# The delta-rule heads' outputs turned by VectorE in 32x32 blocks instead of by TensorE, and attention outputs multiplied by their reciprocals one visit later

## The chip, the core and the metric

The kernel runs on one core of a Trainium2 chip. The metric is the device time of one execution in microseconds (us). The three runs of the kernel before took 1198.80, 1198.78 and 1195.98 us; their median is 1198.78 us.

## The reference, cut to what matters

One decoder layer over 1024 tokens of width 1024, all in float32:

```python
h = rmsnorm(x, norm1_w);  proj = h @ w_in                 # q, k, v, z, gates | q, k, v of attention
o_a = gated_delta_rule(q, k, v, g, beta)                  # 4 heads x 128
o_a = rmsnorm(o_a, gdn_norm_w) * silu(z)
o_b = dilated_attention(q_b, k_b, v_b)                    # 8 heads x 64, numerator / denominator
x = x + concat([o_a, o_b]) @ w_out
h = rmsnorm(x, norm2_w);  u = causal_dwconv(h @ w_up)
x = x + (silu(gate) * up) @ w_down;  out = rmsnorm(x, final_norm_w)
```

The delta rule is a recurrence over chunks of tokens for each of the four heads. Its result `o_a` has tokens on the rows; the output projection wants it with the 128 features of a head on the partitions, so each head's 128 x 1024 result has to be turned once.

## The kernel before, in words

All large matrix products run on TensorE as three products of split operands (high and low parts), each 128x512 out: one "triple" is `xhi,whi`, `xlo,whi`, `xhi,wlo`. The order of TensorE's instructions is the order in which the Python program writes them: every `mm` and `tp` gets an order token. That program is a set of generators (streams) which the class `Weave` interleaves by its own estimate of time: `dense` (level 9, the input projection, the filler), `chain(h)` (level 1, the recurrence of head h), `attention` (level 5), and later `out_proj`, `mlp_up`, `mlp_down`. VectorE, ScalarE, GpSimd and the SyncE queue (SP, which issues nearly all DMAs) have no tokens: there a list scheduler places each instruction where it reckons the engine free and the operands ready, and the order in which the program writes them only ranks what is ready at once. Engines `uv` and `ua` give their instructions a rank 400 places ahead. Every engine then runs its queue in order.

Names used below, with the lines of before:

- `chain(h)` (847): for each of 8 chunks a loop through two engines: `mm(kT, st)`, then VectorE makes `r`, `mm(um, r)`, VectorE makes `wke` and ScalarE copies `w`, `mm(ktok, wke)`, VectorE makes the new state `ct`, and so on. Beside it `vtok` collects the output. All four heads run at once, 0 and 1 ahead of 2 and 3. At the end `ms` (911) is raised to -0.5 on GpSimd, and GpSimd multiplies `vtok` by it (912, 913).
- `finish(h)` (916): turns `vtok` of a head in two halves. Four 128x128 transposes on TensorE go into one bank of PSUM (`tag "atr"`), ScalarE copies the bank to `ot` with the scale `gw2`, and a DMA writes `ot` to the DRAM tensor `mixer`. `ot` has two buffers under the tag `t2`, shared with `oT` and `rT`.
- `dense()` (535): after the values and the q and v columns come eight attention columns `a` and four columns `z`. A column is 16 triples in two halves of eight; each half ends in a bank with tag `hf` (two buffers) which VectorE empties (`aqkv`, 1.10 us). Column `z` of head h waits for `finish(h)` (588), loads `og` back from `mixer` (613) and multiplies it by the gate (614).
- `attention()` (949) waits for all four `finish`. Its work is cut in visits (`advance`, 1095): in a visit the newest pair of blocks is turned (`turn`, 1006: transposes of `sm`, copies to `pt` and `pb`), the pair before it is multiplied with the values, and the next pair's scores go to `softmax` (990: VectorE's fused maximum, ScalarE's exponentials). At every second visit a group is complete; `give` (1080) multiplies its bank `po` with `rT`, the reciprocals of the denominators, which VectorE turned (`dt`, 1035, a 128x32 block transpose) and a DMA through `ddram` spread over the partitions.

Of the kernel before, what the change touches and what calls it, by code (L numbers as in the profile page):

```python
# [7 lines left out]
F32 = mybir.dt.float32  # L8
F32R = mybir.dt.float32r
AF = mybir.ActivationFunctionType  # L10
# [137 lines left out]
def hybrid_layer(tc, I, out):  # L148
# [113 lines left out]
    atpark = dp.tile([H, P, S], F32, name="atpark")  # L262
    ddram = dp.tile([7, 8, P], F32, name="ddram")
    ndram = dp.tile([S], F32, name="ndram")
    xpark = dp.tile([KT, P, S], F32, name="xpark")
    upark = dp.tile([FT, P, S], F32, name="upark")

# [3 lines left out]
    def next_bank(tag, *tiles, slack=0.0):  # L271

        while max(wv.need(*tiles), wv.slot_free(tag, 2)) + slack > 1e-3:
            yield max(wv.need(*tiles), wv.slot_free(tag, 2)) + slack
        return bank(tag)
# [239 lines left out]
    def silu2(xr, name):  # L515
        y = A(name, "ev")
        ac.activation(y, xr, AF.Tanh, scale=0.5)
        ve.scalar_tensor_tensor(y, y, 1.0, xr, op0=OP.add, op1=OP.mult)
        return y
# [15 lines left out]
    def dense():  # L535

        yield from wv.until("first")
        yield from wv.until("norms")
        wv.add(2, first_keys())

        srcs, tiles = [], 0
        for col in DENSE:
            if col[0] == "V":
                srcs += [I["wv"][j] for j in range(4)]
            else:
                srcs.append(I["wi"][tiles])
                tiles += 1
        place = [0]
        raw = [raw_weight(srcs[0])]
        nxt = [weight(None, st=raw.pop())]  # L550
        raw.append(raw_weight(srcs[1]))

        def take():
            w = nxt.pop()
            i = place[0] = place[0] + 1
            if i < len(srcs):
                nxt.append(weight(None, st=raw.pop(), spare=i >= 17))
            if i + 1 < len(srcs):
                raw.append(raw_weight(srcs[i + 1]))
            return w  # L560

        def values_by_token(g):

            banks = [bank(t) for t in ("asc", "asc", "ch", "ch")]
            for j in range(4):
                w = [t.rearrange("p (k m) -> p k m", k=2) for t in take()]
                for kk in range(2):
                    k = 2 * j + kk
                    for i, pt in enumerate(banks):
                        c = 4 * g + i  # L570
                        yield wv.need(pt, *w)
                        mm3(pt, [t[:, c * P:(c + 1) * P] for t in xs[k]], [t[:, kk, :] for t in w], k == 0, k == KT - 1)
            for i in range(0, 4, 2):
                vx = A("vx", "ev", shape=(P, 2, 512))
                for e in range(2):
                    c = 4 * g + i + e
                    ac.activation(vx[:, e, :], banks[i + e], AF.Copy, scale=rst[:, c:c + 1])
                c = 4 * g + i
                sy.dma_start(vpark[c * P:(c + 2) * P].rearrange("(e p) d -> p e d", e=2), vx)
            wv.done.add(("V", g))  # L580

        for i, col in enumerate(DENSE):
            kind, h = col[:2]
            if kind == "V":
                yield from values_by_token(h)
                continue
            if kind == "z":
                yield from wv.until(("o", h))
            w = [t.rearrange("p (k m) -> p k m", k=KT) for t in take()]
            pair = []  # L590
            for hh in range(2):
                pt = bank("hf")
                yield wv.need(pt, *w)
                for k in range(KT):
                    mm3(pt, [t[:, k, :] for t in w], [t[:, half(hh)] for t in xs[k]], k == 0, k == KT - 1)
                    yield 0.0

                pair.append(pt)
                if hh == 0:
                    xr = A("aqkv" if kind == "a" else "xr", "go" if kind == "k" else "ev")  # L600
                scaled(pair, "xr", kind == "a", t=xr, hs=(hh,))
            if kind == "k":
                T["k", h] = conv_silu(xr, 4 + h, "kT", "kT*")
                wv.add(3, kprep(h))
            elif kind == "q":
                q = conv_silu(xr, h, "qT", "qa")
                wv.add(4, qprep(h, q))
            elif kind == "v":
                v = conv_silu(xr, 8 + h, "vT", "qa")
                wv.add(4, vprep(h, v))  # L610
            elif kind == "z":
                og = gated[h] = A("og", "kT*")
                sy.dma_start(og, mixer[h])
                ve.tensor_tensor(og, og, silu2(xr, "zz"), op=OP.mult)
            else:
                sy.dma_start(apark[h, col[2]], xr)
                wv.done.add(col)
        wv.done.add("dense")
# [295 lines left out]
        wv.add(1, finish(h, vtok))  # L914

    def finish(h, osb):
        for hh in range(2):
            pt = yield from next_bank("atr", osb)
            for c in range(4):
                i = 4 * hh + c  # L920
                tp(pt[:, c * P:(c + 1) * P], osb[:, i * P:(i + 1) * P])
            ot = tile_(sp, [P, 512], F32, "ot", "t2", 2)
            ac.activation(ot, pt, AF.Copy, scale=gw2)
            sy.dma_start(mixer[h][:, half(hh)], ot)
        wv.done.add(("o", h))


# [21 lines left out]
    def attention():  # L949
# [56 lines left out]
        def turn(pair):  # L1006
            pts = A("pt", "dv*", shape=(P, 2, 2, 256))
            for b, (it, tag) in enumerate(zip(pair, ("asc", "atr"))):
                sm, near, far, u, den = it["sm"], it["near"], it["far"], it["u"], it["den"]
                nn, nf = near // P, -(-far // P)  # L1010
                pt = it["pt"] = pts[:, b]
                pps = [bank(tag) for _ in range(2)]
                pvs = [pp.rearrange("p (e i t) -> p e i t", e=2, t=64) for pp in pps]
                for e in range(2):
                    for i in range(nn + nf):
                        o = far + i * P if i < nn else (i - nn) * P
                        for pv, rr in zip(pvs, HALVES):
                            tp(pv[:, e, i, :], sm[rr, e, o:o + P], ident[rr, rr], 0.055)
                copies = uv.tensor_copy, lambda dst, src: ua.activation(dst, src, AF.Copy)
                for pv, rr, copy in zip(pvs, HALVES, copies):  # L1020
                    copy(pt.rearrange("p e (i t) -> p e i t", t=P)[:, :, :nn, rr], pv[:, :, :nn, :])
                    for i in range(nf):
                        rows = min(it["far"] - i * P, P)
                        copy(it["pb"][i][:rows, :, u, rr], pv[:rows, :, nn + i, :])
                g = it["g"]
                if g["n"] < 7:
                    uv.reciprocal(dns[g["n"] % 2][:, 2 * u:2 * u + 2], den)
                    continue
                rd = it["rd"] = tile_(sp, [P, P], F32, "rd", ("r0", "r1", "w0", "w1")[u], 1)
                uv.reciprocal(den, den)  # L1030
                po_.tensor_copy(rd.rearrange("p (e d) -> p e d", e=2), den[:, :, None].to_broadcast([P, 2, 64]))
            g = pair[0]["g"]
            if g["n"] < 7 and pair[1]["u"] == 3:
                dt = tile_(sp, [P, 32], F32, "dt", "dt", 2)
                ve.transpose(dt, dns[g["n"] % 2])
                to = ddram[g["n"]]
                for b in range(4):
                    sq.dma_start(to[:, 32 * b:32 * b + 32], dt[32 * b:32 * b + 8, :])
                rT = g["rT"] = tile_(sp, [P, 512], F32, "rT", "t2", 2)
                for e, er in enumerate(HALVES):  # L1040
                    src = to.rearrange("(u e) t -> e u t", e=2)[e]
                    sq.dma_start(rT[er].rearrange("p (u t) -> p u t", u=4),
                                 bass.AP(tensor=src.tensor, offset=src.offset, ap=[[0, 64]] + list(src.ap)))
# [47 lines left out]


        pipe = [None, None]

        def advance(pair):
            older, newer = pipe
# [8 lines left out]
                yield from spread(older)  # L1105
            if newer is not None:
                turn(newer)
            if older is not None:
                yield from values(older)
                if older[1]["u"] == 3:  # L1110
                    yield from merge_classes(g)
                    give(g)
            if pair is not None:
                yield from scores(pair, 0.3 if older is None else SSLACK)
            pipe[:] = newer, pair
# [599 lines left out]
```

## Time and profile before

| what | value |
|---|---|
| median of three runs | 1198.78 us |
| the profiled execution's own time | 1197.6 us |
| its span, first to last instruction | 1195.7 us |
| granted TensorE clock, mean | 0.997 |
| TensorE busy | 1183.4 us, 99% of the span |
| VectorE busy | 914.6 us, 76% |
| ScalarE busy | 571.6 us, 48% |
| DMA moved | 157.20 MB, 131 GB/s |

A timeline row gives start, duration, engine, line, operation, the tiles written and read, and a count; what stands in brackets is idle time before the row and who ended it. Matmuls overlap in the pipeline: a 128x512 product is shown with some 0.39 us, but the next starts 0.23 us after it. What an instruction costs TensorE is therefore read from one start to the next. Lines 142, 144, 194 and 198 are those of the helpers that issue instructions, so rows are told apart by their tiles.

### The profile page before, as it was taken

The page shows a single profiled execution, that of the slowest core. Times are in us where ns is not written, and L with a number is a line of the kernel's source. Part 1 is how long each engine was busy: PE and PEld are TensorE (multiplying, and loading weights), DVE is VectorE, ACT ScalarE, POOL GpSimd, SP SyncE. Part 2 cuts the span into 40 slices and gives each one's busy share as a digit, 9 for nine tenths or more (in the row PEclk, how much of TensorE's full clock was granted, in tenths as well). Part 3 has the DMA queues.
Part 4 walks back from the last instruction along what each step waited for, and adds up shares of the span by engine and source line. Part 5 has one row for each costly group of instructions (what it writes and reads, how often), then busy time and mean ns, then how long its engine had stood idle before and what let it go on. Part 6 is the DMA issues. An engine that isn't in the chain of part 4 may idle for free.

```text
span 1195.7 us, 18250 instructions
## 1 busy us (share of the span) xinstructions
PE 1183.4 (99%) x7014; PEld 977.9 (82%) x7014; DVE 914.6 (76%) x1457; ACT 571.6 (48%) x1119; POOL 81.9 (7%) x74
## 2 busy tenths in 40 slices
PE   9999999999999999999999999999999999999997
PEld 6888888888777778888888888888888888888886
DVE  6683975666365665777898898989889889999875
ACT  7275345355444533655554444445444453434441
POOL 0212010214211110000000000000000000000000
PEclk9999999999999999999999999999999999999998
DMA  7435234435644214443322312132231398546514
GB/s 238 107 96 146 79 118 129 145 120 176 223 133 133 90 49 129 166 159 106 106 79 79 104 55 106 53 106 76 83 104 56 123 359 293 194 153 224 169 53 141
DMA packets 90263, 157.20 MB, mean 131 GB/s; under 512 B 21920, under 2 KB 40640, under 8 KB 90176
## 3 DMA queue, kind: packets, MB, share of 16 engines
q1 hardware_dynamic: 89312, 155.25, 39.8%
q8 instruction: 55, 0.90, 0.3%
q10 hardware_dynamic: 864, 0.79, 0.2%
q14 instruction: 32, 0.26, 0.1%
HBM read 120.04 MB, written 35.96 MB: 130 GB/s over the span
## 4 chain that ended last, share of the span: by engine, by line
PE 95%; ACT 2%; DVE 2%; issue 1%; DMA 0%; POOLq 0%; POOL 0%; DVEq 0%; SPq 0%; ACTq 0%
PE ps L194 45%; PE pa L194 20%; PE dw L194 17%; PE pc L194 10%; PE ps L198 2%; DVE kT L142 1%; ACT sm L144 1%; DMA xt<-in_xT 0%; ACT whi L142 0%; DVE x1h L142 0%; DVE zz L142 0%; ACT dec L142 0%; PE pd L194 0%; DVE xr L142 0%; DVE sm L144 0%
## 5 line engine op out<-in xcount | busy, mean ns | idle before, releaser
L194 PE MATMUL dw<-pr 128*128 128x512 f32 (+1 forms) x984 | 211.9, 377 | 0.0
L194 PEld LDWEIGHTS dw<-pr 128*128 128x128 f32 x984 | 176.5, 188 | 34.4 <-DVE x1h L142 0.4
L194 PE MATMUL ps<-xhi,whi 128*128 128x512 f32 x384 | 157.1, 409 | 1.2 <-ACT xhi L144 1.2
L194 PE MATMUL ps<-xhi,wlo 128*128 128x512 f32 x384 | 150.1, 391 | 0.0
L194 PE MATMUL ps<-xlo,whi 128*128 128x512 f32 x384 | 148.4, 390 | 0.0
L194 PE MATMUL pa<-T,pair 128*128 128x512 f32 x528 | 127.1, 390 | 0.1
L194 PEld LDWEIGHTS pa<-T,pair 128*128 128x128 f32 x528 | 99.0, 188 | 20.9 <-ACT u L142 0.5
L194 PEld LDWEIGHTS ps<-xhi,whi 128*128 128x128 f32 x384 | 72.2, 188 | 20.1 <-issue 5.6
L194 PEld LDWEIGHTS ps<-xhi,wlo 128*128 128x128 f32 x384 | 72.1, 188 | 15.5
L194 PEld LDWEIGHTS ps<-xlo,whi 128*128 128x128 f32 x384 | 72.3, 188 | 12.7 <-DVE xlo L144 0.2
L142 ACT ACTIVATE u<-pa 128x512 f32<-128x512 f32 x44 | 26.3, 599 | 107.8 <-PE pa L194 107.8
L142 DVE SCALAR_TENSOR_TENSOR y<-xu,fcw,y 128x1023 f32<-128x1023 f32 (+1 forms) x44 | 56.4, 1281 | 23.3 <-ACT y L142 23.2
L142 ACT ACTIVATE whi<-wst 128x1024 fp32r<-128x1024 f32 x36 | 38.2, 1062 | 65.2 <-PE ps L194 43.4
L194 PE MATMUL pa<-T,S 128*128 128x512 f32 x264 | 63.5, 389 | 0.0
L194 PE MATMUL pc<-T,S 128*128 128x512 f32 x264 | 63.4, 389 | 0.0
L194 PE MATMUL pa<-B,A 128*128 128x512 f32 x264 | 63.4, 389 | 0.0
L194 PE MATMUL pc<-B,pair 128*128 128x512 f32 x264 | 63.4, 389 | 0.0
L142 ACT ACTIVATE pr<-r 128x1024 fp32r<-128x1024 f32 (+1 forms) x44 | 36.6, 840 | 51.5 <-PE dw L194 29.8
L142 DVE TENSOR_TENSOR wst<-wst 128x512 f32<-128x512 f32 x88 | 60.5, 687 | 0.8
L194 PE MATMUL ps<-B,pair 128*128 128x512 f32 x252 | 60.5, 389 | 0.0
L194 PEld LDWEIGHTS pa<-T,S 128*128 128x128 f32 x264 | 49.5, 188 | 10.5 <-ACT p L142 0.2
L194 PEld LDWEIGHTS pc<-T,S 128*128 128x128 f32 x264 | 49.6, 188 | 10.3
(253 smaller groups left out, 2325.0 us busy)
## 6 DMA issues: line engine op xcount, KB each, us to landing
wst<-in_wu SPq DMA_DIRECT2D x44, 512.0 KB
wd<-in_wd SPq DMA_DIRECT2D x44, 512.0 KB
upark<-y SPq DMA_DIRECT2D x22, 512.0 KB
wst<-in_wi SPq DMA_DIRECT2D x21, 512.0 KB
r<-upark SPq DMA_DIRECT2D x11, 512.0 KB
r<-upark SPq DMA_DIRECT2D x22, 256.0 KB
wa<-in_wd SPq DMA_DIRECT2D x22, 256.0 KB
wst<-in_wv SPq DMA_DIRECT2D x8, 512.0 KB
```

Source lines behind the costliest of these rows:

```text
L142: return getattr(eng, op)(*a, **kw)
L144: return getattr(eng, op)(*a, **kw)
L194: tc.stamp_issue_order_token(nc.tensor.matmul(dst, lhs, rhs, start=start, stop=stop, **kw).ins, TOKEN)
L198: tc.stamp_issue_order_token(nc.tensor.transpose(dst, src, ident if idt is None else idt).ins, TOKEN)
```

## The change

Four edits.

1. `finish` no longer uses TensorE, the bank and ScalarE. VectorE transposes each 128x128 piece of `vtok` in 32x32 blocks (`ve.transpose`) straight to `ot`; four DMAs for each half put the blocks in their places in a new DRAM tensor `odram`, each in 512 runs of 128 B; four DMAs for each head read `og` back in runs of 512 B. The scale `gw2` moves to the gate's multiplication, which becomes a `scalar_tensor_tensor`.
2. `finish` yields until the chains of heads 2 and 3 are written.
3. In `turn`, the rows that make and spread the reciprocals (`dt`, `ddram`, `rT`) become a function `rows_out` of their own.
4. `give` of a group is put on a list and written one visit later, between `turn` and `rows_out`; the last two groups keep their place.

```diff
+    odram = dp.tile([H, 32, 4 * S], F32, name="odram")
...
                 og = gated[h] = A("og", "kT*")
-                sy.dma_start(og, mixer[h])
-                ve.tensor_tensor(og, og, silu2(xr, "zz"), op=OP.mult)
+                of = odram[h].rearrange("j (c a t) -> a j c t", c=NCH, a=4)
+                for a in range(4):
+                    sq.dma_start(v8(og)[32 * a:32 * a + 32], of[a])
+                ve.scalar_tensor_tensor(og, og, gw2, silu2(xr, "zz"), op0=OP.mult, op1=OP.mult)
...
     def finish(h, osb):
+        for i in (2, 3):
+            yield from wv.until(("c", i, NCH - 1))
+        yield wv.need(osb)
         for hh in range(2):
-            pt = yield from next_bank("atr", osb)
+            yield 0.3
+            ot = tile_(sp, [P, 512], F32, "ot", "t2", 2)
             for c in range(4):
-                i = 4 * hh + c
-                tp(pt[:, c * P:(c + 1) * P], osb[:, i * P:(i + 1) * P])
-            ot = tile_(sp, [P, 512], F32, "ot", "t2", 2)
-            ac.activation(ot, pt, AF.Copy, scale=gw2)
-            sy.dma_start(mixer[h][:, half(hh)], ot)
+                ve.transpose(ot[:, c * P:c * P + P], osb[:, (4 * hh + c) * P:(4 * hh + c + 1) * P])
+            to = odram[h].rearrange("j (f b i) -> b j f i", f=32, b=4)[:, :, 16 * hh:16 * hh + 16]
+            for b in range(4):
+                sq.dma_start(to[b], ot[32 * b:32 * b + 32].rearrange("p (f i) -> p f i", i=32))
...
+        def rows_out(pair):
             g = pair[0]["g"]
...
+            while ungiven:
+                give(ungiven.pop())
+            if newer is not None:
+                rows_out(newer)
...
-                    give(g)
+                    if g["n"] < 6:
+                        ungiven.append(g)
+                    else:
+                        give(g)
```

On TensorE the 32 transposes `ps<-ident,vtok` are gone and nothing else is added or removed. The attention's visits stand five triples later among the dense work (its first scores after 275 triples instead of 270), and from the triple numbered 321 on the two orders are the same.

VectorE, where the last chunks of heads 2 and 3 are done (`ps_2456`, and `ps_2457` after the change, is the bank of head 2; `ps_2466` and `ps_2467` that of head 3). Before:

```order
L142 TENSOR_SCALAR ms_2447<-ms_2447 128x8
L144 SCALAR_TENSOR_TENSOR vtok_2413<-ps_2962,gq_2327,vtok_2413 128x128
L142 TENSOR_TENSOR aqkv_2980<-ps_2650,rstdB_245 128x4x32x4
L144 TENSOR_SCALAR wke_2974<-ps_2456,ke_1096 128x128
L144 SCALAR_TENSOR_TENSOR r_2978<-ps_2466,ngam_248,vtok_2413 128x128
```

and after, at the same place (`vtok_1483` is the output of head 0):

```order
L142 TENSOR_SCALAR ms_2448<-ms_2448 128x8
L142 STREAM_TRANSPOSE ot_3151<-vtok_1483 128x128
L144 SCALAR_TENSOR_TENSOR vtok_2414<-ps_2963,gq_2328,vtok_2414 128x128
L142 STREAM_TRANSPOSE ot_3151<-vtok_1483 128x128 x2
L142 TENSOR_TENSOR aqkv_2981<-ps_2651,rstdB_246 128x4x32x4
L142 STREAM_TRANSPOSE ot_3151<-vtok_1483 128x128
L144 TENSOR_SCALAR wke_2975<-ps_2457,ke_1097 128x128
L144 SCALAR_TENSOR_TENSOR r_2979<-ps_2467,ngam_249,vtok_2414 128x128
```

The first four transposes stand ahead of head 2's `wke` and head 3's `r`, though the program writes them after both chains.

VectorE, at the last `ct` and `r` of head 3 (chunk 7). Before:

```order
L144 SCALAR_TENSOR_TENSOR ct_2432<-ct_2432,ge_630,ps_2466 128x128
L144 SCALAR_TENSOR_TENSOR vtok_2413<-ps_3126,gq_2327,vtok_2413 128x128
L144 SCALAR_TENSOR_TENSOR r_3142<-ps_2466,ngam_248,vtok_2413 128x128
L142 TENSOR_TENSOR aqkv_3177<-ps_3106,rstdB_245 128x4x32x4
L144 SCALAR_TENSOR_TENSOR vtok_2413<-ps_3167,gq_2327,vtok_2413 128x128
```

and after (`vtok_2030` is the output of head 2, `vtok_1713` that of head 1):

```order
L142 STREAM_TRANSPOSE ot_3169<-vtok_2030 128x128
L144 SCALAR_TENSOR_TENSOR ct_2433<-ct_2433,ge_631,ps_2467 128x128
L142 STREAM_TRANSPOSE ot_3169<-vtok_2030 128x128 x3
L142 STREAM_TRANSPOSE ot_3181<-vtok_1483 128x128 x4
L144 SCALAR_TENSOR_TENSOR vtok_2414<-ps_3104,gq_2328,vtok_2414 128x128
L142 TENSOR_TENSOR aqkv_3117<-ps_3063,rstdB_246 128x4x32x4
L144 SCALAR_TENSOR_TENSOR r_3115<-ps_2467,ngam_249,vtok_2414 128x128
L142 STREAM_TRANSPOSE ot_3190<-vtok_1713 128x128 x4
L144 SCALAR_TENSOR_TENSOR vtok_2414<-ps_3138,gq_2328,vtok_2414 128x128
```

Seven transposes and an `aqkv` now stand between head 3's last `ct` and its last `r`, and one transpose of head 2's output ahead of that `ct`. On GpSimd a weight's low part (`wlo`) now stands between the power of head 2's `ms` and the multiplication of its `vtok`.

VectorE in the attention, at the first `oT`. Before:

```order
L144 COPY pt_3522<-ps_3542 128x4x64
L144 COPY pb_3400<-ps_3542 128x2x64
L142 TENSOR_TENSOR oT_3577<-ps_3416,rT_3462 128x4x4x32
L144 ISA sm_3596,mx_3597<-ps_3580,mk_2953 128x416
L144 ISA mx_3597 128x1
```

and after:

```order
L144 COPY pt_3546<-ps_3566 128x4x64
L144 COPY pb_3424<-ps_3566 128x2x64
L142 TENSOR_TENSOR oT_3715<-ps_3443,rT_3489 128x4x4x32
L144 ISA sm_3617,mx_3618<-ps_3601,mk_2954 128x416
L144 ISA mx_3618 128x1
```

The multiplication keeps its place in VectorE's queue, between the copies of one visit and the maxima of the same visit; only its tile is numbered later, because it is written later.

More of the change, by code (lines that the diff above doesn't have):

```diff
@@ L1093, in attention @@
         pipe = [None, None]
+        ungiven = []
         def advance(pair):
```

## The prediction

> **What bounds the kernel now.** I read the page first, then the table of windows around the changed stage, then the timelines of TensorE, VectorE and GpSimd in it. From the page, the busy times and the chain that ended last:
>
> ```profile
> PE 1183.4 (99%) x7014; PEld 977.9 (82%) x7014; DVE 914.6 (76%) x1457; ACT 571.6 (48%) x1119; POOL 81.9 (7%) x74
> PE 95%; ACT 2%; DVE 2%; issue 1%; DMA 0%; POOLq 0%; POOL 0%; DVEq 0%; SPq 0%; ACTq 0%
> ```
>
> TensorE is busy 1183.4 of 1195.7 us and holds 95% of the chain, so the time is TensorE's work plus its few waits. The windows of the stage in which the chains end and the attention begins (columns: stretch, length, then busy time and count of each engine, clock, DMA share, GB/s):
>
> ```profile
> 270.00:290.00 20.00, 19.41 (x146) 17.93 (x145) 13.66 (x45) 13.12 (x52) 7.38 (x5) 1.00 0.54 163
> 290.00:310.00 20.00, 20.00 (x109) 17.13 (x108) 6.65 (x15) 7.97 (x20) 10.01 (x7) 1.00 0.73 224
> 310.00:330.00 20.00, 20.00 (x168) 15.27 (x166) 7.61 (x30) 8.99 (x26) 4.75 (x2) 1.00 0.67 231
> ```
>
> TensorE hardly waits here. VectorE (third pair) is busy 13.66, 6.65 and 7.61 of 20 us: it has room for more, but its instructions are steps of the chains for which TensorE waits, so the place of new work counts more than its amount.
>
> **What leaves TensorE.** The 32 transposes stand in six places of TensorE's timeline, each quoted with the row that follows:
>
> ```profile
> 284.48 1.03 PE L198 MATMUL ps<-ident,vtok 128*128 128x128 f32 x8
> 285.35 0.39 PE L194 MATMUL ps<-wke,ktok 128*128 128x128 f32 x2
> ...
> 287.61 0.39 PE L194 MATMUL ps<-w,qat 128*128 128x128 f32 x2
> 288.12 0.63 PE L198 MATMUL ps<-ident,vtok 128*128 128x128 f32 x4
> 288.58 0.39 PE L194 MATMUL ps<-ct,kT 128*128 128x128 f32 x2
> ...
> 289.73 0.60 PE L198 MATMUL ps<-ident,vtok 128*128 128x128 f32 x4
> 290.08 0.48 PE L194 MATMUL ps<-xhi,whi 128*128 128x512 f32 x1
> 290.40 0.40 PE L194 MATMUL ps<-xlo,whi 128*128 128x512 f32 x1
> 290.63 0.40 PE L194 MATMUL ps<-xhi,wlo 128*128 128x512 f32 x1
> ...
> 298.87 0.60 PE L198 MATMUL ps<-ident,vtok 128*128 128x128 f32 x4
> 299.31 0.39 PE L194 MATMUL ps<-ct,kT 128*128 128x128 f32 x2
> ...
> 300.23 0.60 PE L198 MATMUL ps<-ident,vtok 128*128 128x128 f32 x4
> 300.58 0.48 PE L194 MATMUL ps<-xhi,whi 128*128 128x512 f32 x1
> ...
> 310.92 1.03 PE L198 MATMUL ps<-ident,vtok 128*128 128x128 f32 x8
> 311.71 0.48 PE L194 MATMUL ps<-xhi,whi 128*128 128x512 f32 x1
> ```
>
> From start to start: 0.87, 0.46, 0.35, 0.44, 0.35, 0.79, together 3.26. Where a 128x512 product follows, its own pace is spoiled too: 290.08 to 290.40 is 0.32, against 0.23 for the next, so 0.09 goes with each of the three places where the transposes alone broke a run of triples: 0.27. And ahead of 288.12 stands a wait: the pair before it started at 287.61 and such a pair takes 0.22 (285.35 ends a run in which pairs follow at that pace), so 0.29 goes. The sum is 3.82 us, all of it on the path. It would be no gain only where TensorE waits in its place, which is the next term. ScalarE's eight copies of `ot` go too; ScalarE is busy 7.97 of 20 us there, so I count nothing for them.
>
> **What VectorE gets.** 32 transposes of 128x128. The trace has none of that size; the nearest is the one of 128x32, and steps of the chain show what a 128x128 operation takes. VectorE's and GpSimd's timelines, around the first and the second place of the order:
>
> ```profile
> L142 DVE STREAM_TRANSPOSE dt<-dn x7: 211/211/213, 328.5 to 417.4; 128x32 f32<-128x32 f32 x7
> 283.54 1.10 DVE L142 TENSOR_TENSOR aqkv<-ps,rstdB 128x512 f32<-128x512 f32 x1
> 284.48 0.33 DVE L144 TENSOR_SCALAR wke<-ps,ke 128x128 f32<-128x128 f32 x1
> 284.72 0.34 DVE L144 SCALAR_TENSOR_TENSOR r<-ps,ngam,vtok 128x128 f32<-128x128 f32 x1
> ...
> 298.63 0.35 DVE L144 SCALAR_TENSOR_TENSOR ct<-ct,ge,ps 128x128 f32<-128x128 f32 x1 [1.26 <-PE ps L194]
> 299.74 0.34 DVE L144 SCALAR_TENSOR_TENSOR r<-ps,ngam,vtok 128x128 f32<-128x128 f32 x1
> 281.26 1.90 POOL L142 TENSOR_TENSOR vtok<-vtok,ms 128x1024 f32<-128x1024 f32 x1
> 293.13 1.64 POOL L142 TENSOR_TENSOR ms<-ms,mhalf 128x8 f32<-128x8 f32 x1 [1.24 <-DVE ms L142]
> 296.70 2.38 POOL L142 TENSOR_TENSOR wlo<-wst,whi 128x1024 fp32r<-128x1024 f32 x1
> ```
>
> A transpose lies between 0.21 (a quarter of the columns) and 0.84 (four times that). I take 0.26 from start to start: 128x128 operations follow each other after 0.24 (284.48 to 284.72), and the 128x32 transpose with its 0.211 is already near them. The Trainium skill, "VectorE: DVE Perf Modes", section "The three transpose paths", gives 311 ns on VectorE and 390 ns on TensorE for a 128x128 bf16 transpose; by 0.31 the waits below would grow by 16 x 0.05 = 0.8 us.
>
> First place: head 0's `vtok` is ready at 281.26 + 1.90 = 283.16, as VectorE gets there. Four transposes push `wke` from 284.48 to 285.52, and it ends at 285.52 + 0.33 = 285.85. TensorE now has two triples before the product that needs it. With a triple of 3 x 0.23 and 0.09 for the change of kind they take 1.45 from 283.70, where such a product starts in before's timeline, so TensorE arrives at 285.15 and **waits 0.7 us** (from 0, if transposes take 0.21 and the ends overlap, to 1.9, if GpSimd's rough span ends as late as the transposes at 284.48 allow).
>
> ```profile
> 283.56 0.39 PE L194 MATMUL ps<-ct,kT 128*128 128x128 f32 x2
> 283.70 0.47 PE L194 MATMUL ps<-xhi,whi 128*128 128x512 f32 x1
> ```
>
> Next come four transposes ahead of head 3's `ct`; with two triples on TensorE before the product that reads it, I find `ct` done as TensorE arrives: 0.
>
> Second place: head 2's multiplication on GpSimd now comes after a `wlo`: 293.13 + 1.64 + 2.38 + 1.90 = 299.05. The one transpose ahead of `ct` waits for it, and `ct` starts at about 299.5 instead of 298.63; TensorE, which has more triples in front, reads it at 300.1 and does not notice. But between `ct` and `r` stand seven transposes, a `vtok` and an `aqkv`: 0.26 + 7 x 0.26 + 0.26 + 0.94 (283.54 to 284.48) = 3.28, and `r` ends 0.35 later, 3.63 after `ct` starts. TensorE has its pair (0.14) and three triples (3 x 0.68 + 0.09 = 2.13) from 300.1, so it wants `r` at 302.4 and gets it at 303.15: it **waits 0.8 us** (0 to 2.5, by transposes of 0.21 and of about half the upper price).
>
> After that no chain is left. TensorE has 22 triples (15 us) before the first scores, and the remaining 16 transposes, 4.2 us, lie beside them. What they can hold up there is `aqkv`, which frees the bank that TensorE needs eight triples (5.4 us) later. That cover is gone only if the transposes themselves wait, which is a rival below.
>
> **DMA queue.** SP issues 32 + 16 DMAs instead of 8 + 4. The nearest shapes, in runs of 128 B:
>
> ```profile
> 173.94 1.91 SPq L142 DMA_DIRECT2D x<-xdram  x4
> 175.96 3.88 SPq L142 DMA_DIRECT2D um<-xtdram  x8
> 300.70 0.38 SPq L142 DMA_DIRECT2D wst<-in_wi  x1
> 322.12 1.04 ACT L142 ACTIVATE whi<-wst 128x1024 fp32r<-128x1024 f32 x1
> ```
>
> At 0.48 each that is 36 x 0.48 = 17 us more of SP's time between 285 and 330. Behind them are weights: the one loaded at 300.70 is first read at 322.12, so a delay of some us there is covered by 20 us. `og` is read only after 410 us. I count 0.
>
> **Later multiplication.** The order shows `oT` unmoved in VectorE's queue, so this part does not do what it says; 0. What moves in the attention is ScalarE's `whi`: it stood between two exponentials of a visit in which TensorE then waited, and stands now between two of another visit.
>
> ```profile
> PE ps L198 <- ACT sm L144: 0.8, 4, 0.2
> ```
>
> These waits are 0.8 us in all. I take 0, with bounds of 0.8 on both sides.
>
> **Sum.** -3.82 + 0.7 + 0.8 = -2.3 us. Against the profiled execution (1197.6 with a span of 1195.7, 1.9 us lying around it) that makes 1195.3. The median of the runs is 1198.78, 1.2 above the profiled one; from it, **1196.5 us**, 0.19% faster. That is less than 0.3% (3.6 us), about what a measurement of this kernel can tell from no change.
>
> **Rivals.** *VectorE has the slack* (faster). If the transposes slip into gaps, none of the two waits comes and the four waits on exponentials go as well: -3.82 - 0.8 = -4.6, 1194.2. For it: VectorE's 6.65 us of 20 busy. Against it: the order puts them ahead of chain steps, and in order they run. With the waits halved it is -3.1, just short of the bound.
>
> *VectorE becomes the chain's bound* (slower). Four transposes stand before `wke`, four before a `ct`, eight before the last `r`, so each 0.1 us more for one costs up to 1.6. At 0.26 + 2.3/16 = 0.40 the gain is gone; at 0.63 the kernel is 3.6 slower; at 0.84 it is 16 x 0.58 - 2.3 = +7.0, 1205.8. Against it: 0.211 for 128x32, most of which must be fixed, since operations of 128x128 take 0.33 to 0.35. In the same page of the skill, "Rules for kernel authors" sends 128x128 transposes to TensorE where PSUM will do; TensorE did it here, 8 of them in 0.87 us.
>
> *The small runs land late.* `ot` has two buffers, so the fifth and sixth groups of transposes wait for the DMAs of the third and fourth. VectorE stands still meanwhile, and `ms` and `aqkv` are behind. SP issues these 16 DMAs in a row from about 301 (their place behind the `wst` at 300.70), the fourth group's until 301 + 8 x 0.48 = 304.9. After landing come four transposes (1.0), `ms` (0.2) and `aqkv` (1.1); TensorE needs that bank eleven triples (7.5) after its last chain product at about 305, so at 312.5. Landing later than 312.5 - 304.9 - 2.3 = 5.3 us after issue delays TensorE one for one.
>
> ```profile
> 313.16 0.40 SPq L142 DMA_DIRECT2D mixer<-ot  x1
> 318.57 0.32 SPq L142 DMA_DIRECT2D og<-mixer  x1
> ```
>
> In before the read had to wait for the write: 5.0 us from the end of issue, with larger transfers in front. At 8 us it would cost 2.7, 1199.2, the same within what can be told. The skill's page warns that plain DMAs with strided patterns for a transpose are 19 times slower than its crossbar; no run here shows that.
>
> **Chances.** The forecast with its bounds and the late landing 0.60 of no difference; slack on VectorE 0.31 of faster; VectorE as the bound 0.09 of slower. The range takes the faster rival, 1194.2, less 0.7 because runs of before alone lie 2.8 us apart, and at the top the upper bounds of the two waits, -3.82 + 1.9 + 2.5 = +0.6, with 0.8 in the attention: 1200.2. So 1193.5 to 1200.2.
>
> **What would show it.** Right: no `ident,vtok` on TensorE, `STREAM_TRANSPOSE ot<-vtok` about 0.3 us long, TensorE waiting on DVE `wke` and DVE `r` in the stage of the chains for 0.5 to 1 us each, waits on `sm` about as before, the rest of the span unchanged. Wrong: transposes above 0.4 us, VectorE idle on DMA `odram<-ot` with TensorE waiting for `aqkv`, or first scores later or earlier by more than a us than the sum says.

## The result, and the profile after

The changed kernel took 1201.87 us (median of ten runs, 1200.51 to 1202.99), the kernel before on the same chip 1197.43 us (median of ten, 1195.98 to 1201.06): a ratio of 1.0034 (the medians alone give 1.0037), with a 95% interval from 1.0025 to 1.0043. It is slower, by about 4 us, and above the range that was forecast. The profiled execution has a span of 1200.2 us and a mean granted clock of 0.994.

The page of the changed kernel, busy times and the chain that ended last:

```profile
PE 1182.8 (99%) x6982; PEld 977.1 (81%) x6982; DVE 920.5 (77%) x1489; ACT 566.9 (47%) x1111; POOL 81.2 (7%) x74
PE 92%; DVE 2%; DMA 2%; ACT 2%; issue 1%; SPq 0%; POOLq 0%; POOL 0%; DVEq 0%; ACTq 0%
```

TensorE has 32 instructions less and is busy as long as before; its share of the chain fell from 95% to 92%, and a DMA, which had none, now holds 2%. The windows of the changed kernel say where (columns as before: stretch, length, busy time and count of PE, PEld, DVE, ACT and POOL, clock, DMA share, GB/s):

```profile
290.00:310.00 20.00, 20.00 (x104) 16.80 (x103) 9.66 (x31) 5.87 (x18) 7.75 (x6) 1.00 0.70 165
310.00:330.00 20.00, 20.00 (x163) 15.18 (x161) 10.27 (x38) 7.98 (x24) 6.94 (x4) 1.00 0.89 207
330.00:350.00 20.00, 15.22 (x199) 11.33 (x197) 8.21 (x30) 7.63 (x25) 2.18 (x2) 0.91 0.51 143
350.00:400.00 50.00, 50.00 (x628) 38.67 (x627) 28.71 (x107) 23.59 (x82) 6.72 (x8) 0.97 0.52 149
```

Until 330 us TensorE is as full as before. Then it stands for 4.8 of 20 us, in the first visits of the attention, and its clock falls to 0.91 and 0.97. The DMA engines are busier ahead of that: 0.89 from 310 to 330 us, where before had 0.67.

**The chains.** Measured at the dense products that both kernels run, the changed kernel wins 2.7 us between 270 and 311 us. TensorE at the first place of the order, VectorE at both places, and TensorE at the second:

```profile
284.43 0.40 PE L194 MATMUL ps<-xhi,wlo 128*128 128x512 f32 x1
285.36 0.49 PE L194 MATMUL ps<-wke,ktok 128*128 128x128 f32 x2 [0.53 <-ACT w L144]
...
302.01 0.40 PE L194 MATMUL ps<-xhi,wlo 128*128 128x512 f32 x1
302.24 0.44 PE L194 MATMUL ps<-r,um 128*128 128x128 f32 x2
```

```profile
284.48 0.28 DVE L142 STREAM_TRANSPOSE ot<-vtok 128x128 f32<-128x128 f32 x1
284.68 0.32 DVE L144 TENSOR_SCALAR wke<-ps,ke 128x128 f32<-128x128 f32 x1
...
299.26 1.47 DVE L142 STREAM_TRANSPOSE ot<-vtok 128x128 f32<-128x128 f32 x7
...
301.81 0.32 DVE L144 SCALAR_TENSOR_TENSOR r<-ps,ngam,vtok 128x128 f32<-128x128 f32 x1
```

From 284.43 to 285.36 is 0.93 where the next product follows after 0.23: a wait of 0.70. What ends it is ScalarE's copy `w`, which reads the same bank as `wke` and starts as that ends: it runs from 285.03 to 285.31. At the second place 302.01 to 302.24 is 0.23: no wait. Seven transposes take 1.47, of which the last one's own 0.27, so 0.20 from one to the next.

**The first visits.** SP's timeline of the changed kernel, with most other rows left out; the row before the last is the first group's reciprocals on their way out, the last row their way back:

```profile
300.28 11.03 SPq L142 DMA_DIRECT2D odram<-ot  x16
...
318.42 7.96 SPq L142 DMA_DIRECT2D odram<-ot  x8
...
327.65 2.73 SPq L142 DMA_DIRECT2D og<-odram  x4
...
333.57 2.90 SPq L142 DMA_DIRECT2D ddram<-dt  x4
339.98 1.29 SPq L142 DMA_DIRECT2D rT<-ddram  x2
```

The same two steps in the kernel before:

```profile
328.74 1.34 SPq L142 DMA_DIRECT2D ddram<-dt  x4
331.58 1.86 SPq L142 DMA_DIRECT2D rT<-ddram  x2
```

VectorE has turned `dt` at 328.5 us in both kernels. SP comes to it 4.8 us later, takes 1.56 longer over four writes of 1 KB, and after the last of them 3.51 us pass until the read can go (339.98 - 336.47) instead of 1.50: together 8.4 us. The chain that ended last (start, duration, what) says what the last two of these are:

```profile
330.43 5.77 DMA wst<-in_wi
336.21 3.65 DMA ddram<-dt
340.65 2.95 DMA rT<-ddram
344.10 1.06 DVE oT L142
```

SP issues the first three of the four writes about as in before. The fourth stands 1.4 us until the load of a weight, `wst` of 512 KB, has landed, which SP issued among the last pieces. In the traces the DMAs raise eight semaphores (counters of what has landed) in turn, and each DMA is issued only when the one eight places ahead of it, which raised the same semaphore, has landed; for the fourth write that is `wst`. The fourth write then lands 3.65 us after its issue, where before's took 1.66. What this weight alone is worth was not tried. What the late reciprocals do on VectorE, ScalarE and TensorE in the changed kernel:

```profile
344.10 1.06 DVE L142 TENSOR_TENSOR oT<-ps,rT 128x512 f32<-128x512 f32 x1 [7.74 <-DMA rT<-ddram]
345.00 0.57 DVE L144 CUSTOM_DVE_ANT_0 sm<-ps,mk 128x416 f32<-128x416 f32 x1
```

```profile
345.68 0.64 ACT L144 ACTIVATE sm<-sm,mx 128x416 f32<-128x416 f32 x1 [9.46 <-DVE mx L144]
```

```profile
342.21 0.39 PE L194 MATMUL ps<-xhi,wlo 128*128 128x512 f32 x1
346.47 1.32 PE L198 MATMUL ps<-ident,sm 64*128 64x64 f32 x16 [3.87 <-ACT sm L144]
348.69 1.35 PE L198 MATMUL ps<-ident,sm 64*128 64x64 f32 x16 [0.91 <-ACT sm L144]
349.97 1.97 PE L194 MATMUL ps<-pt,vn 128*64 128x128 f32 x16
351.87 1.64 PE L194 MATMUL ps<-kT,qT 64*128 64x128 f32 x8
353.44 0.50 PE L194 MATMUL ps<-xhi,whi 128*128 128x512 f32 x1
```

VectorE stands 7.74 us at `oT`, which waits for `rT`. The maxima of the visit are ready to run, but stand behind `oT` in VectorE's queue; ScalarE's exponentials wait for the maxima, and TensorE's transposes of `sm` for those: 3.87 and 0.91 us. Short windows of the changed kernel show that it doesn't end there (the column ahead of the last two is the clock):

```profile
344.00:346.00 2.00, 0.00 (x0) 0.00 (x0) 1.91 (x4) 0.32 (x1) 0.00 (x0) 1.00 0.01 4
346.00:348.00 2.00, 1.32 (x16) 0.98 (x16) 2.00 (x7) 2.00 (x6) 0.00 (x0) 0.63 0.35 131
350.00:352.00 2.00, 2.00 (x20) 1.67 (x18) 1.16 (x6) 0.70 (x3) 0.47 (x1) 0.50 0.22 82
354.00:356.00 2.00, 2.00 (x16) 1.43 (x16) 0.57 (x4) 1.10 (x4) 0.00 (x0) 1.00 0.94 372
```

After the wait TensorE runs at half its clock until about 353 us.

Along TensorE the whole sum is this. Ahead of 140 us, where the program is the same, the two traces differ by 0.5 us. From there to the end the changed kernel wins 2.7 us in the chains, loses 7.1 in the attention (7.8 in this visit, less 0.7 elsewhere), and loses 1.0 at 973 us in a wait for `xu`, of which 0.3 comes back: 5.1 in all. That the wait at 973 us comes of the change isn't shown.

### The profile page after: what moved, and what is told of

Same layout as the page of the kernel before. It is cut to its first block, busy times and chain, and to the rows that moved or that the text cites. A ratio compares the mean times of both kernels' runs of the same rounds, so it can differ in the third digit from the quotient of the medians.

```text
span 1200.2 us, 18256 instructions
## 1 busy us (share of the span) xinstructions
PE 1182.8 (99%) x6982; PEld 977.1 (81%) x6982; DVE 920.5 (77%) x1489; ACT 566.9 (47%) x1111; POOL 81.2 (7%) x74
## 4 chain that ended last, share of the span: by engine, by line
PE 92%; DVE 2%; DMA 2%; ACT 2%; issue 1%; SPq 0%; POOLq 0%; POOL 0%; DVEq 0%; ACTq 0%
PE ps L194 43%; PE pa L194 20%; PE dw L194 17%; PE pc L194 10%; PE ps L198 2%; DMA r<-upark 1%; DVE kT L142 1%; ACT sm L144 1%; DMA wst<-in_wi 0%; SPq L142 0%; DMA xt<-in_xT 0%; DMA ddram<-dt 0%; DMA rT<-ddram 0%; DVE x1h L142 0%; ACT whi L142 0%
## 5 line engine op out<-in xcount | busy, mean ns | idle before, releaser
L142 DVE SCALAR_TENSOR_TENSOR y<-xu,fcw,y 128x1023 f32<-128x1023 f32 (+1 forms) x44 | 56.4, 1281 | 23.3 <-ACT y L142 23.2
L144 ACT ACTIVATE sm<-sm,mx 128x128 f32<-128x128 f32 (+7 forms) x64 | 35.5, 556 | 50.2 <-DVE mx L144 50.2
```

Source lines behind the costliest of these rows:

```text
L142: return getattr(eng, op)(*a, **kw)
L144: return getattr(eng, op)(*a, **kw)
```

## The experiments

Two theories. **S**: the small pieces in which `ot` is now written and `og` read (48 DMAs instead of 12) hold up the reciprocals; `oT` then blocks VectorE, TensorE waits, and its clock falls. **V**: the 32 transposes on VectorE, among the steps of the chains, cost the time; the DMAs are beside the path. All ratios are to the kernel before on the same chip, with their 95% intervals.

### The reads of og later

```diff
-                    sq.dma_start(v8(og)[32 * a:32 * a + 32], of[a])
+                    after(sq.dma_start(v8(og)[32 * a:32 * a + 32], of[a]), last["rT"], "the reciprocals go first")
```

(and `last["rT"]` is set where `rT` is read.)

> The changed kernel, with the 32 reads of og (four per head) held behind the reads of the reciprocals, so that SP issues them later; the 32 small-run writes stay in place. Theory S: SP reaches the first ddram<-dt some 8 x 1.0 = 8 us earlier or as many of the og reads as stood ahead of it, rT lands as in the kernel before, the 4.8 us wait goes, ratio 0.998. If the writes alone are enough of a backlog, part of the wait stays, 1.000 to 1.003. Theory V: no change, 1.0034.

There are 16 of these reads, four for each of the four heads, not 32.

Measured: 1192.96 us, ratio 0.9961 (0.9949 to 0.9972). SP's timeline and TensorE's, in the run with the reads later:

```profile
328.67 1.34 SPq L142 DMA_DIRECT2D ddram<-dt  x4
331.03 1.28 SPq L142 DMA_DIRECT2D rT<-ddram  x2
```

```profile
342.15 0.39 PE L194 MATMUL ps<-xhi,wlo 128*128 128x512 f32 x1
342.47 1.21 PE L198 MATMUL ps<-ident,sm 64*128 64x64 f32 x32
343.61 1.09 PE L194 MATMUL ps<-pt,vn 128*64 128x128 f32 x16
344.63 1.00 PE L194 MATMUL ps<-kT,qT 64*128 64x128 f32 x8
345.56 0.50 PE L194 MATMUL ps<-xhi,whi 128*128 128x512 f32 x1
```

The reciprocals are as early as in the kernel before, and the visit takes TensorE 3.41 us (342.15 to 345.56) where the changed kernel takes 11.23 (342.21 to 353.44): 7.8 us, of which 4.8 are the two waits and 3.0 the half clock (1.97 for 1.09 and 1.64 for 1.00 in two of its groups). The gain is larger than the expected 0.998: from 140 us on, this trace wins 4.1 us on before's, 2.8 in the chains, 0.8 in the attention (0.4 of it in waits on `sm`) and 0.5 behind 970 us. S holds, V falls: the transposes are where they were.

### The first outputs really one visit later

```diff
+            inst = ve.tensor_tensor(oT.rearrange("p (n u c) -> p n c u", n=4, c=4), *by, op=OP.mult)
+            if g["n"] < 6:
+                after(inst, last["copy"], "the copies of the next visit go first")
```

(`last["copy"]` is VectorE's latest copy in `turn`.) SP's queue is untouched.

> The changed kernel, with the first six oT really one visit later in VectorE's queue (behind the copies of the next visit's turn); SP's queue is not touched, so the reciprocals land as late as in the changed kernel, near 344 us. Theory S: VectorE no longer stands at oT ahead of the maxima of the same visit; TensorE's wait on sm falls from 4.8 to below 1 us although the DMA is as late, ratio 0.998. Theory V: no change, 1.0034. A third reading, that the late DMA costs by itself whatever waits for it, gives 1.003 too.

Measured: 1193.17 us, 0.9962 (0.9950 to 0.9974). VectorE and SP in this run:

```profile
338.60 0.59 DVE L144 CUSTOM_DVE_ANT_0 sm<-ps,mk 128x416 f32<-128x416 f32 x1 [2.42 <-PE ps L194]
...
344.70 1.06 DVE L142 TENSOR_TENSOR oT<-ps,rT 128x512 f32<-128x512 f32 x1
```

```profile
332.67 2.74 SPq L142 DMA_DIRECT2D ddram<-dt  x4
338.92 1.29 SPq L142 DMA_DIRECT2D rT<-ddram  x2
```

The reciprocals are nearly as late as in the changed kernel (read at 338.92 against 339.98), and it costs nothing: `oT` runs at 344.70, almost when it ran there, but the maxima went ahead at 338.60 instead of 345.00. So the late DMA alone isn't the loss; it is the late DMA at the head of a queue with other work behind it.

### Both

The edits of both runs together.

> The changed kernel with both repairs: the reads of og behind the reciprocals, and the first six oT one visit later in VectorE's queue. Each alone gave 0.996. Theory S: both take away the same wait, so together they give 0.996 again, not 0.992. If each had taken away a cost of its own, 0.993 or less.

Measured: 1193.58 us, 0.9964 (0.9952 to 0.9976). They take away the same wait; either is enough.

### The reciprocals on ScalarE's queue

```diff
+    sr = Engine(wv, nc.scalar, "small", 0.05, 0.00036, 0.4)
...
-                    sq.dma_start(to[:, 32 * b:32 * b + 32], dt[32 * b:32 * b + 8, :])
+                    sr.dma_start(to[:, 32 * b:32 * b + 32], dt[32 * b:32 * b + 8, :])
```

(and the same for the reads of `rT`.)

> The changed kernel, with the writes of the turned reciprocals (ddram<-dt) and their reads (rT<-ddram) issued by ScalarE instead of SP. Theory S (the reciprocals stand behind a backlog of 128-byte-run DMAs on SP; VectorE's queue stands at the first oT ahead of the maxima, so TensorE waits 4.8 us for sm and its clock is lower afterwards): rT lands by about 337 us instead of 344, the waits of TensorE on sm fall to about 1 us, and the ratio to the kernel before is 0.998. If not SP's queue but the busy DMA engines hold the reciprocals up, the first oT still waits for rT by 1 to 5 us and the ratio is between 1.000 and 1.003. Theory V (the 32 transposes on VectorE cost their time ahead of chain steps; the DMAs are beside the path): no change, 1.0034.

Measured: 1204.58 us, 1.0051 (1.0038 to 1.0064), worse than the changed kernel and against every expectation. ScalarE's timeline in this run:

```profile
332.01 0.27 ACTq L142 DMA_DIRECT2D ddram<-dt  x1
...
335.90 0.27 ACTq L142 DMA_DIRECT2D ddram<-dt  x1
339.20 1.32 ACTq L142 DMA_DIRECT2D rT<-ddram  x2
340.62 0.59 ACT L144 ACTIVATE sm<-sm,mx 128x352 f32<-128x352 f32 x1 [7.76 <-issue]
```

The writes and reads are hardly earlier (339.20 against 339.98), and now it is ScalarE's queue that stands, 7.76 us, with the exponentials behind. So a place of its own in an issuing queue doesn't make these DMAs fast while the pieces are in flight (DMA share 0.95 from 310 to 330 us). Each of the four writes still waits until the DMA eight places ahead, one of SP's, has landed: three for a read of `og`, and the fourth, issued at 335.90, for the weight `wst`, which lands at 335.88. Then 3.0 us pass from the last write to the read (339.20 - 336.17), against 3.51 in the changed kernel and 1.50 in before. The Trainium skill, "DMA: Bandwidth & Descriptors", section "Issuing engines are not separate DMA queues", says that DMAs started by different engines run on the same 16 DMA engines and interleave, and that a second issuing engine saves only the time of issue. This run agrees as far as the landing goes.

### Plain rows

The changed kernel's transposes, but `ot` goes to `mixer` in one DMA for each half and `og` comes back in one for each head, as before.

```diff
-            for b in range(4):
-                sq.dma_start(to[b], ot[32 * b:32 * b + 32].rearrange("p (f i) -> p f i", i=32))
+            sy.dma_start(mixer[h][:, half(hh)], ot)
```

> The changed kernel with its transposes on VectorE, but with ot written by one plain 128x512 DMA to mixer and og read by one plain 128x1024 DMA, as in the kernel before; it leaves out that the four blocks of each transpose are put in their places, so the layout of the output is not the reference's. Theory S: 12 instead of 48 DMAs, the reciprocals as early as in the kernel before, no wait at the first oT, ratio 0.997 to 0.998, the gain that the chains show (2.7 us) left over. Theory V: the transposes on VectorE are unchanged, so 1.0034.

Measured: 1196.02 us, 0.9988 (0.9979 to 0.9996). The long wait is gone (TensorE's longest wait on `sm` is 0.3 us) with the transposes in place, against V; but the gain falls short of the expected 0.997 to 0.998 and is a third of that with the reads later. Between those two traces 3.6 us differ: 1.0 ahead of 140 us, where nothing differs in the program; about 1.1 in visits, which stand among other triples here; 0.9 at 573 us, in a wait for `p`; and 0.5 at 973 us. What causes these differences stays open.

### The small pieces without the transposes

The kernel before with the changed kernel's DMAs alone: the same lines as above, the other way round.

> The kernel before with TensorE's transposes and ScalarE's copies as they were; only ot is written and og read in the changed kernel's small pieces (32 + 16 DMAs instead of 8 + 4). The blocks aren't turned inside, so the layout isn't the reference's. Theory S (the DMAs alone hold the reciprocals up): rT lands after 340 us instead of 335, TensorE waits for sm by 2 to 5 us, and the ratio lies between 1.002 and 1.006; if SP gets through its pieces before dt is turned at 328 us, there is no wait and 1.000, which would say that the place of the pieces in SP's queue decides and not their number. Theory V: 1.000.

Measured: 1204.53 us, 1.0049 (1.0030 to 1.0068), with runs from 1199.21 to 1207.05. The pieces alone cost what S says; V's 1.000 falls. The profiled execution is the fastest of them and shows a mild case: `oT` waits 4.22 us for `rT`, TensorE's longest wait for `sm` is 0.8, and the mean clock is 0.998. The three slowest runs (1205.84 to 1207.05) have mean clocks of 0.994 and 0.995. That the clock makes the difference between them fits, but their traces were not taken.

### The other part alone

The kernel before with the later writing of `give` (edits 3 and 4).

```diff
+            while ungiven:
+                give(ungiven.pop())
...
-                    give(g)
+                    if g["n"] < 6:
+                        ungiven.append(g)
```

> The kernel before with the other part of the change alone: the multiplications by the reciprocals are written one visit later, the transposes stay on TensorE. The order that comes of it differs from the kernel before in seven rows of SP's queue only; oT stands where it stood on VectorE. Theory S: the reciprocals land in time, nothing is gained and nothing lost, 1.000. Had this part any effect of its own, the ratio would leave 1.000 by more than 0.001.

Measured: 1197.61 us, 1.0001 (0.9992 to 1.0010). This part does nothing, as the order said.

### How late is too late

The kernel before, with k more DMAs on SP ahead of the first reciprocals, and the maxima of that visit held behind the first `oT`, where they stand in the kernel before as well:

```diff
+                if g["n"] == 0:
+                    for i in range(k):
+                        nc.sync.dma_start(spill[i], dt[:8, :])
```

k = 14:

> As the runs with 20 and 30 more writes in the kernel before (1.0049 and 1.0097), with 14: rT lands about 2.2 us earlier than with 20, near 341.5 us, so that TensorE's longest wait for sm is 0.5 to 1 us instead of 2.8. If the clock falls only after the longer waits, the windows show 1.00 throughout and the ratio is 1.000 to 1.002, less than half of the 1.0049. If each us of delay costs the same whatever its place, 1.0034.

k = 20:

> The kernel before, with the first oT held ahead of the maxima of its visit on VectorE, and 20 more writes of 1 KB (spill<-dt, never read) on SP right ahead of the first ddram<-dt. At 0.335 us each (the four of ddram<-dt took 1.34) they make rT land 6.7 us later, at about 342 us. Theory S: the first 5 us of that are free, TensorE waits 1.5 to 2.5 us for sm, its clock stays at 1.00, and the time grows by the wait alone: 1.0015 to 1.002. If the clock falls after any wait, 1.004. Theory V, by which the late reciprocals cost nothing: 1.000.

k = 30:

> As the run with 20 writes, but with 30: rT lands 10 us later than in the kernel before, at about 345 us. TensorE waits about 5 us for sm. If the late reciprocals cost their delay alone, 10 writes more cost 3.35 us more than 20 do, and the ratio is 1.0045. If TensorE's clock then stands at 0.5 for some 6 us, as it did after the wait in the changed kernel, some 3 us come on top: 1.007. Theory V: 1.000.

| k | `rT` issued at (us) | longest wait of TensorE on `sm` (us) | ratio |
|---|---|---|---|
| 14 | 335.49 | 0.2 | 1.0009 (0.9999 to 1.0020) |
| 20 | 339.50 | 2.8 | 1.0049 (1.0037 to 1.0061) |
| 30 | 340.74 | 4.8 | 1.0097 (1.0082 to 1.0112) |

The trace with 20 runs 1.2 us behind the other two here. From the first added write to the read of `rT` it is 7.1, 10.0 and 12.5 us. TensorE with k = 20, behind its wait:

```profile
346.15 0.46 PE L198 MATMUL ps<-ident,sm 64*128 64x64 f32 x8 [2.82 <-ACT sm L144]
...
348.63 1.97 PE L194 MATMUL ps<-pt,vn 128*64 128x128 f32 x16
350.53 1.44 PE L194 MATMUL ps<-kT,qT 64*128 64x128 f32 x8
```

and with k = 14:

```profile
343.77 0.47 PE L198 MATMUL ps<-ident,sm 64*128 64x64 f32 x8 [0.19 <-ACT sm L144]
344.17 1.09 PE L194 MATMUL ps<-pt,vn 128*64 128x128 f32 x16
345.19 1.14 PE L194 MATMUL ps<-kT,qT 64*128 64x128 f32 x8
```

With 14 the wait on the DMA lies beside the dense triples, and the clock stays; the wait on `sm` is shorter than the 0.5 to 1 us expected. With 20 the expectation of 1.002 was missed: the clock falls after 2.8 us too (1.97 for 1.09), and the visit costs 5.6 us. The price isn't proportional: 1.1 us for 14, 5.9 for 20, 11.6 for 30, where the last ten writes hold SP only 2.5 us longer (10.13 against 7.60). With 30 the expectation of 1.007 was missed too. Its profiled execution lost 7.9 us in the visit and was the fastest of its runs; what the others lost beyond that is open. The Trainium skill, "TensorE: Matmul & The Clock Gate", section "Part 1: The HAM clock gate (the "warmup" mystery)", has the clock at half after one idle window of about 3.4 us and back after one busy window, the windows running freely. The half clock agrees (0.50 in the changed kernel), and so do its lengths, one to three times some 3.4 us: 6.8 us in the changed kernel and with k = 30, 3.4 with k = 20, and 10.2 with the reciprocals on ScalarE's queue. But a wait shorter than a window was enough: with k = 20 TensorE stood 2.8 us, ran again from 346.15 with gaps of 0.2 us, and the clock fell at 348.2. So one shouldn't count on 3.4.

### The transposes behind the chains

The reads of `og` later, and every transpose behind the last `r`:

```diff
+                after(inst, last["r"], "the chains go first")
```

> The changed kernel with og read late (0.996) and, besides, all 32 transposes held behind the last r of the chains on VectorE. Theory S: the wait of 0.69 us for wke at the first place goes; if nothing new waits, 0.9955. Theory V, that transposes among the chains cost more than that one wait: 0.993 or less. Against both: the 32 transposes then stand in a row ahead of aqkv, and those after the eighth wait for the ot ring of two buffers; if the DMAs of ot land more than 5 us after issue, TensorE waits for a bank at about 312 us, and the ratio is above 0.996.

Measured: 1192.90 us, 0.9964 (0.9952 to 0.9976), no different from the reads later alone. From the dense product ahead of `wke` to the one behind it TensorE takes 0.69 us less than there, so that wait was the transposes' doing; the span is only 0.2 shorter, since 0.4 us came back in a wait for `xu` at 969 us. V's 0.993 falls here too. VectorE waits for the two buffers of `ot`, up to 1.5 us at a time, and TensorE doesn't notice.

## Why the prediction was wrong, point by point

- **TensorE's loss of work, right.** 3.82 us less 0.70 of waits is 3.1; the stage of the chains shows 2.7. Where the other 0.4 went I did not trace.
- **First place, right in size, in part by luck.** 0.7 forecast, 0.70 measured, and 0.69 given back when the transposes were moved. But `wke` was done only 0.34 us after TensorE stood at the product (285.00 against 284.66), not 0.7; the rest is ScalarE's copy `w` behind it, for which the forecast had no term.
- **Second place, wrong in size.** 0.8 forecast, 0 measured. Transposes follow each other after 0.20 us instead of the 0.26 that I took, and the `ct` ahead of them started at 299.00 instead of 299.5; so `r` ends at 302.13, in time for the product at 302.24. The error made the forecast too slow, not too fast.
- **DMA queue, the step that failed.** "Behind them are weights [...] I count 0." Two things went wrong. First the size: 32 writes take 23.3 us of SP (rows of 1.95, 2.31, 11.03 and 7.96) and 16 reads 10.1, together 33, where 48 at my 0.48 make 23. One write took 0.50 in the median (0.30 to 1.65) and one read 0.61, so the price of a write was about right; what I left out is that SP also stands between them. Second, and decisive: I named the weights and `og` as what stands behind, and not the next thing with a short way to TensorE, the reciprocals, which stand behind them in the same queue at 328.7 us. Instead of 0 this cost TensorE 7.8 us. A weight among them was not harmless either: the fourth write of the reciprocals waited 1.4 us for its landing.
- **Later multiplication, right and read wrongly.** `oT` is unmoved, and that part alone measures 1.0001. But this was the warning: an unmoved `oT` stands ahead of the maxima, so what delays `rT` delays TensorE. I took 0.8 us as the bound for the waits in the attention; they became 5.2, and the half clock came on top, for which the prediction had no term at all.
- **VectorE has the slack.** With the late reciprocals out of the way the change measures 0.9961 and 0.9962, about 1194.1 us on the median of 1198.78, close to this rival's 1194.2. That is luck, since it comes by another sum: the first wait is there, the second isn't, and of the 0.8 us on exponentials 0.4 goes.
- **VectorE becomes the bound, wrong.** Its price was 0.40 us per transpose; one takes 0.20.
- **The small runs land late.** The mechanism was near: DMAs of small runs, late. The place was wrong. VectorE did wait for the ring of `ot`, 4.4 us in two waits, and TensorE's triples covered it, as the cover of 7.5 us said they might. The late landing that cost was that of another tensor.

## What to carry to other kernels

When a change adds DMAs to a queue, list everything that is issued on that queue until its backlog is gone, and for each follow the way to the critical engine: a transfer of 1 KB can be the dearest. An in-order engine turns a late operand into a late everything; the remedy is to put the waiting instruction behind work that is ready, or to hold the bulk DMAs behind the small one (a gain of 0.7% here by either), and not to move the DMA to another queue whose engine has work on the path. Price a wait of TensorE of some us with what follows it at half clock.

## What the runs showed of the hardware

- A write in 512 runs of 128 B took SP 0.50 us in the median, close to the 0.48 of a quieter stage; but 32 of them held SP for 23.3 us and 16 reads for 10.1.
- A 1 KB write was issued 1.4 us late because a 512 KB load, issued 5.8 us before it, had not landed; it then took 3.65 us to land, where the same write took 1.66 in before.
- Seven 128x128 float32 transposes on VectorE follow each other every 0.20 us.
- A wait of 3.87 us on TensorE was followed by 6.8 us at a clock of 0.50, and one of 2.8 us by 3.4 us of it.
